# First norm ahead of the embedding projection, output projection beside the last attention blocks, token scales by a three-column chain

## The chip, the cores and the metric

The kernel runs on one core of one Trainium2 chip. The metric is the device time of one execution in microseconds. A core has five engines with an instruction queue each: TensorE (PE) for matmuls, with its weight loads shown apart as PEld; VectorE (DVE); ScalarE (ACT); GpSimd (POOL); and SyncE (SP), which here only issues DMA transfers. They wait for one another through semaphores. Sixteen DMA engines move data between the memory and the core's on-chip buffers. PE writes into PSUM banks; here the large products rotate through one pool of banks (`mm`) and statistics, broadcasts and attention through another (`sm`).

## The reference

One layer of a decoder over 1024 prompt tokens and 32 sample tokens (8 sequences of 4), width 1024, all in float32:

```python
x = x + 0.5 * _swiglu(_rms(x, g1), w1g, w1u, w1d)          # width 1024 -> 2816 -> 1024
z = _rms(x, gm) @ w_in                                     # q | k | v | gate B | gate C | h
q, k = _rms(q, qn), _rms(k, kn)                            # per head of 64
att = sliding window attention (128), 8 query heads, 2 key heads, bias table, sinks
cv  = w_conv[0]*u[t-2] + w_conv[1]*u[t-1] + w_conv[2]*u[t],   u = gate_c * h
x = x + concat([att, gate_b * cv]) @ w_out
x = x + 0.5 * _swiglu(_rms(x, g2), w2g, w2u, w2d)
x = x + sigmoid(_rms(x, gp) @ wpg) * (pe @ wpp)            # pe: embedding of width 256 per token
# _rms(x, g) = x * rsqrt(mean(x*x over the 1024 features) + 1e-6) * g
```

The outputs are x, the last keys and values, and the last two inputs of the convolution.

## The kernel before, in words

Features lie on the 128 partitions in eight tiles `X[0]` to `X[7]`, tokens along the free axis: 1056 columns. So a norm needs a sum over partitions, which PE makes with a matmul against a vector of ones, and its result, one scale for each token, has to be spread over all partitions again. Every float32 operand of a large product is split into a high part (an ACT copy that rounds) and a low part (a DVE subtraction), and a product is three matmuls, high by high, low by high, high by low. The lines 306 to 308 do this for the projections and the down products, 412 to 414 for the gate/up products, 499 to 501 for the first groups of those, 810 to 812 for the embedding projection, 1216 to 1218 for the convolution's columns.

The stages follow one another on PE:

- 0 to 50 us: the embedding projection `pe @ wpp` (`pe_group`, line 806, with PSUM copied out on ACT and DVE, lines 814 and 816); its result is stored and read again at the end. In this stage x is loaded (line 830, one chunk of 528 tokens at a time, two chunks) and chunk 0 is normed: `n_square` (ACT squares x, DVE and POOL add them up, lines 530 to 535), `n_stat` (statistic matmuls on line 548, a chain of small operations for the inverse root on DVE, `small_chain`, lines 232 to 245, broadcast matmuls on line 558, ACT copies on line 559), `n_y` (DVE scales x, line 572, and splits it, lines 334 and 335).
- 50 to 130 us: the first gate/up groups with ordinary products (`lead_group`), fed by chunk 0; the norm of chunk 1 runs beside them as a list of steps, one or two behind each half group. Chunk 1 enters with the third lead group.
- to 520 us the gate/up product by a scheme of seven half-size products, to 795 us the down product.
- 775 to 875 us: the input projection for q, k and v; from here on the tokens are in three chunks (384, 384, 288). Its scales come from `norm_r` (line 281): one statistic matmul per chunk that leaves the sum on all 128 partitions (line 286), and the inverse root on DVE in two halves of the chunk. The same function makes the scales of the final gate at the end.
- 875 to 1117 us: the columns of the convolution (`proj2`), between whose halves the tasks of the sample attention and of the attention blocks 0 to 7 are put by a counter (`half`): scores (1053, 1056), softmax on DVE, ACT and POOL (last operation 1083 on POOL), transposes (1091), product with the values (1100).
- to 1204 us: the output projection (`out_group`, line 1303), its sum with x on DVE (1307). Then the second gate/up (to 1670 us), the second down product (to 1930), and the gate of the embedding with its tanh (`ple`, from line 1362).

An order is written out by hand for each stage; work that is to lie beside another is put in a list by `after(d, fn)`, and `tick()`, called behind each group, runs what is due. `need(flag)` runs the list until a flag is set, `drain()` runs all of it. Weights of the projections pass through two raw buffers (`URAW`) and four split ones: `tick` also splits the next unit as soon as a place is free, and each split starts the load of the next unit on SP. The mixed values (`mix`) of a chunk are split by `split_mix` when its attention blocks are done.

Of the kernel before, what the change touches and what calls it, by code (L numbers as in the profile page):

```python
# [7 lines left out]
F32 = mybir.dt.float32  # L8
# [62 lines left out]
UAT = [40960, 14848, 31680, 33728]  # L71
URAW = [43008, 44032]
# [5 lines left out]
def tile_decoder_layer(  # L78
# [67 lines left out]
    def pump_dma():  # L146
        while st["dma"] < st["end"] and st["dma"] < st["split"] + RAW:
            i = st["dma"]
            t = at("wraw", URAW[i % 2], 1024)
            nc.sync.dma_start(out=t, in_=units[i])  # L150
            raws[i] = t
            st["dma"] += 1
# [128 lines left out]
    def norm_r(c, name, s, d=2):  # L281
        W = CW[c]

        def stat():
            ps = psb(sm)
            nc.tensor.matmul(ps[:, :W], lhsT=ones.broadcast_to([P, P]), rhs=accs[c][:, :W], start=True, stop=True)
            ms = wtile("ms")
            t = wtile("nt")
            rb = rb_of(name, s)[:, CS[c]:CS[c] + W]
            with tc.high_priority(offset=1):  # L290
                nc.vector.tensor_scalar(out=ms[:, :W], in0=ps[:, :W], scalar1=1.0 / D, scalar2=EPS, op0=ALU.mult, op1=ALU.add)
                halves = [slice(0, W // 2), slice(W // 2, W)]
                rsqrt_chain(*[(ms[:, h], rb[:, h], t[:, h]) for h in halves])
            flags.add((name, c))

        after(d, stat)
# [527 lines left out]
    pe_load(praw, psrc, t0_)  # L824
    pe_split(qraw, qh, ql, s0)
    pe_split(praw, ph, pl, t0_)
    pe_load(praw, psrc, t1_)
    pe_load(qraw, wsrc, s1)
    for k in range(KT):
        nc.sync.dma_start(out=chunk(k, 0), in_=xin[:, k, 0:HC])  # L830
    for m in range(4):
        pe_group(m, 0)
    pe_split(praw, ph, pl, t1_)
    for m in range(4):
        pe_group(m, 1)
    pe_split(qraw, qh, ql, s1)
    for k in range(KT):
        n_square(0, k)
    lw1 = lead_weights(w1gu, 0)
    for k in range(KT):  # L840
        nc.sync.dma_start(out=chunk(k, 1), in_=xin[:, k, HC:NT])
    steps0 = chunk0_steps(G1)
    for m in range(4, 8):
        for c in range(2):
            pe_group(m, c)
            if m > 4 and steps0:
                steps0.pop(0)()
    while steps0:
        steps0.pop(0)()

    def chunk1_steps(g, squares):
        s = [lambda k=k: n_square(1, k) for k in range(KT)] if squares else []
        s.append(lambda: n_stat(1))
        return s + [lambda kp=kp, j=j: n_y(1, kp, g, j) for j in range(2) for kp in range(2)]
# [24 lines left out]
    gate_up(w1gu, G1, lw1, chunk1_steps(G1, True), at_end)  # L879
# [4 lines left out]
    mix = [at("mix", KT * CS[c], KT * CW[c]).rearrange("p (k w) -> p k w", k=KT) for c in range(3)]  # L884
# [6 lines left out]
    vsm = at("vsm", 45056, P, rows=NS)  # L891
# [406 lines left out]
    drain()  # L1298
    for k in range(KT):
        nc.sync.dma_start(out=X[k], in_=xm_d[:, k])  # L1300
# [7 lines left out]

    steps0 = chunk0_steps(G2)
    lw2 = None  # L1310
    for c in range(3):
        for m in range(KT):
            out_group(m, c)
            if c == 2:
                wdone(UO + m)
            tick()
            if c == 1:
                n_square(0, m)
                nc.sync.dma_start(out=xs_d[:, m, 0:HC], in_=X[m][:, 0:HC])
            if c == 2:  # L1320
                n_square(1, m)
                nc.sync.dma_start(out=xs_d[:, m, HC:NT], in_=X[m][:, HC:NT])
                if steps0:
                    steps0.pop(0)()
                if m == 4:
                    lw2 = lead_weights(w2gu, 0)
# [19 lines left out]
    gate_up(w2gu, G2, lw2, chunk1_steps(G2, False), dp.early)  # L1346
# [146 lines left out]
```

## Time and profile before

| | |
|---|---|
| median of 3 runs | 2033.95 us (2030.67 to 2036.55) |
| profiled execution | 2031.85 us |
| its span | 2029.9 us, mean granted PE clock 0.984 |
| PE busy | 1986.7 us, 98% of the span, 14051 matmuls |
| DVE, ACT, POOL busy | 1066.5 (53%), 653.2 (32%), 479.3 us (24%) |
| chain of waits that ended last | PE 93%, DVE 5%, ACT 1%, issue 1%, DMA 1% |

The time of the execution is 1.95 us above the span, which runs from the first to the last recorded instruction. Busy time is that of recorded instructions; a busy PE may still run at the lower of its two clocks, which the column of the granted clock tells (1.00 is 2.4 GHz, 0.50 is 1.2 GHz). A row of a timeline can hold several equal instructions (x8); its length then spans all of them.

### The profile page before, as it was taken

The page shows a single profiled execution, that of the slowest core. Times are in us where ns is not written, and L with a number is a line of the kernel's source. Part 1 is how long each engine was busy: PE and PEld are TensorE (multiplying, and loading weights), DVE is VectorE, ACT ScalarE, POOL GpSimd, SP SyncE. Part 2 cuts the span into 40 slices and gives each one's busy share as a digit, 9 for nine tenths or more (in the row PEclk, how much of TensorE's full clock was granted, in tenths as well). Part 3 has the DMA queues.
Part 4 walks back from the last instruction along what each step waited for, and adds up shares of the span by engine and source line. Part 5 has one row for each costly group of instructions (what it writes and reads, how often), then busy time and mean ns, then how long its engine had stood idle before and what let it go on. Part 6 is the DMA issues. An engine that isn't in the chain of part 4 may idle for free.

```text
span 2029.9 us, 34765 instructions
## 1 busy us (share of the span) xinstructions
PE 1986.7 (98%) x14051; PEld 1939.6 (96%) x14051; DVE 1066.5 (53%) x2057; ACT 653.2 (32%) x1334; POOL 479.3 (24%) x414
## 2 busy tenths in 40 slices
PE   7999999999999999999998899999999999999999
PEld 7899999999999999998885899999999999999989
DVE  6745555555524228366684357555555563152474
ACT  5323333334303223323353133333333341042311
POOL 2343343332000122012231025233333310002200
PEclk8999999999999999999997999999999999999999
DMA  7122332221812215111010521223222246121331
GB/s 262 51 84 82 93 115 85 75 85 63 319 56 76 75 60 157 35 30 44 24 30 11 180 86 56 82 86 92 78 82 74 78 145 243 43 76 44 99 106 50
DMA packets 90356, 183.27 MB, mean 90 GB/s; under 512 B 13537, under 2 KB 34921, under 8 KB 90068
## 3 DMA queue, kind: packets, MB, share of 16 engines
q1 hardware_dynamic: 88436, 176.96, 26.5%
q0 software_dynamic: 1472, 4.00, 0.7%
q8 instruction: 110, 1.80, 0.4%
q14 instruction: 50, 0.41, 0.1%
q10 hardware_dynamic: 288, 0.10, 0.0%
HBM read 138.70 MB, written 44.02 MB: 90 GB/s over the span
## 4 chain that ended last, share of the span: by engine, by line
PE 93%; DVE 5%; ACT 1%; issue 1%; DMA 1%; POOL 0%; SPq 0%; ACTq 0%; POOLq 0%; DVEq 0%
PE ps L412 13%; PE ps L413 13%; PE ps L414 13%; PE ps L306 12%; PE ps L307 12%; PE ps L308 12%; PE ps L1217 2%; PE ps L1218 2%; PE ps L1216 2%; PE ps L501 2%; PE ps L499 2%; PE ps L500 2%; PE ps L1056 1%; DVE bl_a L335 1%; PE ps L1053 1%; PE ps L1100 1%
## 5 line engine op out<-in xcount | busy, mean ns | idle before, releaser
L413 PE MATMUL ps<-bh_a,wl_a 128*128 128x264 f32 x2128 | 603.7, 284 | 0.0
L412 PE MATMUL ps<-bh_a,wh_a 128*128 128x264 f32 x2128 | 602.2, 284 | 0.0
L414 PE MATMUL ps<-bl_a,wh_a 128*128 128x264 f32 x2128 | 597.7, 284 | 0.0
L412 PEld LDWEIGHTS ps<-bh_a,wh_a 128*128 128x128 f32 x2128 | 399.9, 188 | 0.6 <-issue 0.6
L413 PEld LDWEIGHTS ps<-bh_a,wl_a 128*128 128x128 f32 x2128 | 399.8, 188 | 0.0
L414 PEld LDWEIGHTS ps<-bl_a,wh_a 128*128 128x128 f32 x2128 | 399.0, 189 | 0.0
L307 PE MATMUL ps<-hh_a,dwl_a 128*128 128x384 f32 (+1 forms) x1056 | 338.8, 321 | 0.0
L306 PE MATMUL ps<-hh_a,dwh_a 128*128 128x384 f32 (+1 forms) x1056 | 337.7, 321 | 0.0
L308 PE MATMUL ps<-hl_a,dwh_a 128*128 128x384 f32 (+1 forms) x1056 | 337.7, 321 | 0.0
L308 PEld LDWEIGHTS ps<-hl_a,dwh_a 128*128 128x128 f32 x1056 | 198.5, 188 | 0.0
L306 PEld LDWEIGHTS ps<-hh_a,dwh_a 128*128 128x128 f32 x1056 | 198.3, 188 | 0.0
L307 PEld LDWEIGHTS ps<-hh_a,dwl_a 128*128 128x128 f32 x1056 | 198.0, 188 | 0.0
L732 DVE SCALAR_TENSOR_TENSOR x_a<-ps,x_a 128x384 f32<-128x384 f32 (+1 forms) x96 | 50.2, 523 | 274.9 <-PE ps L308 270.9
L306 PE MATMUL ps<-xnh_a,whi_a 128*128 128x384 f32 (+1 forms) x528 | 175.2, 332 | 10.5 <-issue 5.7
L307 PE MATMUL ps<-xnh_a,wlo_a 128*128 128x384 f32 (+1 forms) x528 | 172.9, 327 | 1.4 <-DVE wlo_a L161 1.4
L308 PE MATMUL ps<-xnl_a,whi_a 128*128 128x384 f32 (+1 forms) x528 | 172.9, 327 | 0.0
L262 POOL TENSOR_TENSOR acc_a<-acc_a,sq 128x384 f32<-128x384 f32 (+1 forms) x42 | 51.6, 1228 | 436.2 <-ACT sq L261 436.2
L334 ACT CAST wh_a<-ws_a 128x512 fp32r<-128x512 f32 x152 | 94.5, 622 | 155.8 <-PE ps L414 146.4
L335 DVE TENSOR_TENSOR wl_a<-ws_a,wh_a 128x512 fp32r<-128x512 f32 x152 | 107.9, 710 | 58.9 <-ACT wh_a L334 54.2
L335 DVE TENSOR_TENSOR wl_a<-wr_a,wh_a 128x512 fp32r<-128x512 f32 x114 | 105.9, 929 | 30.0 <-ACT wh_a L334 26.3
L306 PEld LDWEIGHTS ps<-xnh_a,whi_a 128*128 128x128 f32 x528 | 101.8, 193 | 14.1 <-issue 7.6
L359 POOL TENSOR_TENSOR ws_a<-wr_a,wr_a 128x512 f32<-128x512 f32 x38 | 52.3, 1377 | 257.9 <-DMA wr_a<-in_w2gu_dram 122.2
(228 smaller groups left out, 3373.2 us busy)
## 6 DMA issues: line engine op xcount, KB each, us to landing
hd<-g_a SPq DMA_DIRECT2D x88, 264.0 KB
wr_a<-in_w1gu_dram SPq DMA_DIRECT2D x88, 256.0 KB
wr_a<-in_w2gu_dram SPq DMA_DIRECT2D x88, 256.0 KB
hr_a<-hd SPq DMA_DIRECT2D x88, 192.0 KB
dwr_a<-in_w1d_dram SPq DMA_DIRECT2D x16, 704.0 KB
dwr_a<-in_w2d_dram SPq DMA_DIRECT2D x16, 704.0 KB
wraw_a<-in_win_dram SPq DMA_DIRECT2D x18, 512.0 KB
hr_a<-hd SPq DMA_DIRECT2D x44, 144.0 KB
```

The lines of the kernel that those rows point to most:

```text
L262: nc.gpsimd.tensor_tensor(out=accs[c], in0=accs[c], in1=sq[:, :W], op=ALU.add)
L306: nc.tensor.matmul(ps[:, :W], lhsT=wh, rhs=xh, start=(k == 0), stop=False)
L307: nc.tensor.matmul(ps[:, :W], lhsT=wl, rhs=xh, start=False, stop=False)
L308: nc.tensor.matmul(ps[:, :W], lhsT=wh, rhs=xl, start=False, stop=(k == n - 1))
L334: nc.scalar.copy(out=hi, in_=src)
L335: nc.vector.tensor_tensor(out=lo, in0=src, in1=hi.bitcast(F32), op=ALU.subtract)
L359: add(out=s[0], in0=r[2], in1=r[3], op=ALU.add)
L412: nc.tensor.matmul(ps[:, :HH], lhsT=wh[:, ks], rhs=bh, start=(start and k == 0), stop=False, skip_group_check=True)
L413: nc.tensor.matmul(ps[:, :HH], lhsT=wl[:, ks], rhs=bh, start=False, stop=False, skip_group_check=True)
L414: nc.tensor.matmul(ps[:, :HH], lhsT=wh[:, ks], rhs=bl, start=False, stop=last, skip_group_check=True)
L499: nc.tensor.matmul(ps[:, :HH], lhsT=wh[:, ks], rhs=bh, start=first, stop=False)
L732: nc.vector.scalar_tensor_tensor(out=x, in0=ps[:, :W], scalar=0.25, in1=x, op0=ALU.mult, op1=ALU.add)
```

## The change

Three things are changed, and buffers are moved for the last of them.

At the start, the eight loads of chunk 0's x are issued ahead of the second half of the embedding operands, every second one from ACT's queue instead of SP's; the squares and the statistic of chunk 0 come ahead of the embedding groups, the scaling of chunk 0 between them; the squares and the sum of chunk 1 come behind the embedding groups and ahead of the lead groups, where they were steps beside the lead groups, and the statistic of chunk 1 (`n_stat(1)`) is the first step.

In `norm_r`, which serves the input projection and the final gate, the sum over partitions now goes to three columns (one matmul for each 128 tokens, tokens on partitions), the inverse root is taken on those three columns by `small_chain`, and three matmuls against the identity and one ACT copy spread the result over all partitions.

At the output projection, `drain()` gives way to `need` for chunk 0 and 1 of the mixed values; the groups run in the order (m 0 to 3, c 0), (0 to 3, c 1), (4 to 7, c 0), (4 to 7, c 1), then chunk 2; x is loaded for m 0 to 4 ahead and for m 5 to 7 before the fifth group. The mixed values of chunk 2, the raw and split weight buffers and one small buffer have new places.

```diff
@@ -68,8 +68,10 @@
     [8448 + 768 * k for k in range(8)],
     [16896 + 576 * k for k in range(8)],
 ]
-UAT = [40960, 14848, 31680, 33728]
-URAW = [43008, 44032]
+UAT = [40512, 14848, 31680, 33728]
+URAW = [42560, 43584]
+URAW2 = [6144, 7168]
+MIXAT = [0, 3072, 42560]
 SLOT = [21504 + 1056 * i for i in range(9)] + [46720, 47776]
 WOUT2 = [21504 + 2048 * i for i in range(4)]
 
@@ -146,7 +148,7 @@
     def pump_dma():
         while st["dma"] < st["end"] and st["dma"] < st["split"] + RAW:
             i = st["dma"]
-            t = at("wraw", URAW[i % 2], 1024)
+            t = at("wraw", (URAW2 if 2 <= i < 26 else URAW)[i % 2], 1024)
             nc.sync.dma_start(out=t, in_=units[i])
             raws[i] = t
             st["dma"] += 1
...
         def stat():
-            ps = psb(sm)
-            nc.tensor.matmul(ps[:, :W], lhsT=ones.broadcast_to([P, P]), rhs=accs[c][:, :W], start=True, stop=True)
-            ms = wtile("ms")
-            t = wtile("nt")
-            rb = rb_of(name, s)[:, CS[c]:CS[c] + W]
-            with tc.high_priority(offset=1):
-                nc.vector.tensor_scalar(out=ms[:, :W], in0=ps[:, :W], scalar1=1.0 / D, scalar2=EPS, op0=ALU.mult, op1=ALU.add)
-                halves = [slice(0, W // 2), slice(W // 2, W)]
-                rsqrt_chain(*[(ms[:, h], rb[:, h], t[:, h]) for h in halves])
+            p2 = psb(sm)
+            ms = small.tile([P, 3], F32, name="pms", tag="pms")
+            r = small.tile([P, 3], F32, name="pr", tag="pr")
+            nc.vector.memset(ms, 1.0)
+            for i, o, n in tiles_of(c):
+                nc.tensor.matmul(p2[:n, i:i + 1], lhsT=accs[c][:, o:o + n], rhs=ones, start=True, stop=True)
+            nf = 3 if c < 2 else 2
+            nc.vector.tensor_scalar(out=ms[:, :nf], in0=p2[:, :nf], scalar1=1.0 / D, scalar2=EPS, op0=ALU.mult, op1=ALU.add)
+            if nf < 3:
+                nc.vector.tensor_scalar(out=ms[:NS, 2:3], in0=p2[:NS, 2:3], scalar1=1.0 / D, scalar2=EPS, op0=ALU.mult, op1=ALU.add)
+            small_chain(ms, r, 3)
+            p3 = psb(sm)
+            for i, o, n in tiles_of(c):
+                nc.tensor.matmul(p3[:, o:o + n], lhsT=r[:n, i:i + 1].broadcast_to([n, P]), rhs=ident[:n, :n], start=True, stop=True)
+            nc.scalar.copy(out=rb_of(name, s)[:, cols(c)], in_=p3[:, :W])
             flags.add((name, c))
 
         after(d, stat)
@@ -822,36 +830,35 @@
     t0_, t1_ = slice(0, HC), slice(HC, NT)
     pe_load(qraw, wsrc, s0)
     pe_load(praw, psrc, t0_)
+    for k in range(KT):
+        (nc.scalar if k % 2 else nc.sync).dma_start(out=chunk(k, 0), in_=xin[:, k, 0:HC])
+    pe_load(praw, psrc, t1_)
+    pe_load(qraw, wsrc, s1)
     pe_split(qraw, qh, ql, s0)
     pe_split(praw, ph, pl, t0_)
-    pe_load(praw, psrc, t1_)
-    pe_load(qraw, wsrc, s1)
+    steps0 = chunk0_steps(G1)
     for k in range(KT):
-        nc.sync.dma_start(out=chunk(k, 0), in_=xin[:, k, 0:HC])
+        n_square(0, k)
+    steps0.pop(0)()
     for m in range(4):
         pe_group(m, 0)
     pe_split(praw, ph, pl, t1_)
+    while steps0:
+        steps0.pop(0)()
+    lw1 = lead_weights(w1gu, 0)
+    for k in range(KT):
+        nc.sync.dma_start(out=chunk(k, 1), in_=xin[:, k, HC:NT])
     for m in range(4):
         pe_group(m, 1)
     pe_split(qraw, qh, ql, s1)
-    for k in range(KT):
-        n_square(0, k)
-    lw1 = lead_weights(w1gu, 0)
-    for k in range(KT):
-        nc.sync.dma_start(out=chunk(k, 1), in_=xin[:, k, HC:NT])
-    steps0 = chunk0_steps(G1)
     for m in range(4, 8):
         for c in range(2):
             pe_group(m, c)
-            if m > 4 and steps0:
-                steps0.pop(0)()
-    while steps0:
-        steps0.pop(0)()
-
-    def chunk1_steps(g, squares):
-        s = [lambda k=k: n_square(1, k) for k in range(KT)] if squares else []
-        s.append(lambda: n_stat(1))
-        return s + [lambda kp=kp, j=j: n_y(1, kp, g, j) for j in range(2) for kp in range(2)]
+    for k in range(KT):
+        n_square(1, k)
+
+    def chunk1_steps(g):
+        return [lambda: n_stat(1)] + [lambda kp=kp, j=j: n_y(1, kp, g, j) for j in range(2) for kp in range(2)]
 
     def mid_hook(m, c):
         square(c, m)
...
-    mix = [at("mix", KT * CS[c], KT * CW[c]).rearrange("p (k w) -> p k w", k=KT) for c in range(3)]
+    mix = [at("mix", MIXAT[c], KT * CW[c]).rearrange("p (k w) -> p k w", k=KT) for c in range(3)]
 
...
-    drain()
-    for k in range(KT):
-        nc.sync.dma_start(out=X[k], in_=xm_d[:, k])
+    def load_xm(ks):
+        for k in ks:
+            nc.sync.dma_start(out=X[k], in_=xm_d[:, k])
...
+    need(("mx", 0))
+    need(("mx", 1))
+    load_xm(range(5))
     steps0 = chunk0_steps(G2)
     lw2 = None
-    for c in range(3):
-        for m in range(KT):
-            out_group(m, c)
-            if c == 2:
-                wdone(UO + m)
-            tick()
-            if c == 1:
-                n_square(0, m)
-                nc.sync.dma_start(out=xs_d[:, m, 0:HC], in_=X[m][:, 0:HC])
-            if c == 2:
-                n_square(1, m)
-                nc.sync.dma_start(out=xs_d[:, m, HC:NT], in_=X[m][:, HC:NT])
-                if steps0:
-                    steps0.pop(0)()
-                if m == 4:
-                    lw2 = lead_weights(w2gu, 0)
+    order = [(m, c) for m0 in (0, 4) for c in (0, 1) for m in range(m0, m0 + 4)] + [(m, 2) for m in range(KT)]
+    for m, c in order:
+        if (m, c) == (0, 1):
+            while st["split"] < 26:
+                split_one()
+            load_xm(range(5, KT))
+        out_group(m, c)
+        if c == 2:
+            wdone(UO + m)
+        tick()
+        if c == 1:
+            n_square(0, m)
+            nc.sync.dma_start(out=xs_d[:, m, 0:HC], in_=X[m][:, 0:HC])
+        if c == 2:
+            n_square(1, m)
+            nc.sync.dma_start(out=xs_d[:, m, HC:NT], in_=X[m][:, HC:NT])
+            if steps0:
+                steps0.pop(0)()
+            if m == 4:
+                lw2 = lead_weights(w2gu, 0)
...
```

The engines' queues move at three places. The first is ACT's queue at the start, before. The names: `wpp` and `pe` (raw `praw`) are the operands of the embedding projection, `po` its result, `x` the activations, `acc` and `sq` their squares, `wh` high parts of the first gate/up weights.

```order
L797 CAST wpph_a_109<-wppr_a_107 128x512
L797 CAST wpph_a_110<-wppr_a_108 128x512
L797 CAST peh_a_103<-praw_a_101 128x528
L797 CAST peh_a_104<-praw_a_102 128x528
L797 CAST peh_a_103<-praw_a_101 128x528
L797 CAST peh_a_104<-praw_a_102 128x528
L797 CAST wpph_a_109<-wppr_a_107 128x512
L797 CAST wpph_a_110<-wppr_a_108 128x512
L814 COPY po_a_113<-ps 128x264
L814 COPY po_a_114<-ps 128x264
L530 ACTIVATE acc<-x_a_72 128x528 x2
L814 COPY po_a_115<-ps 128x264
```

The same place after:

```order
L834 DMA x_a_72<-in_xT_dram 128x528 x4
L805 ACT_TABLE_LOAD
L805 CAST wpph_a_109<-wppr_a_107 128x512
L805 CAST wpph_a_110<-wppr_a_108 128x512
L805 CAST peh_a_103<-praw_a_101 128x528
L805 CAST peh_a_104<-praw_a_102 128x528
L538 ACTIVATE acc<-x_a_72 128x528 x2
L541 ACTIVATE sq<-x_a_72 128x528 x6
L805 CAST peh_a_103<-praw_a_101 128x528
L805 CAST peh_a_104<-praw_a_102 128x528
L822 COPY po_a_113<-ps 128x264
L822 COPY po_a_114<-ps 128x264
```

ACT now issues four loads of x, and the eight squares stand behind four casts and ahead of the four others; before, they stood behind all eight and between the evictions of the first results.

The second place is PE's queue ahead of the transposes (`ident`, `S_a`) of attention block 6, with the buffers' numbers. Before; `ps_10980` is the output group m 3 of chunk 0:

```order
L308 MATMUL ps_10980<-xnl_a45568_6958,whi_a14848_7870 128x384
L306 MATMUL ps_10980<-xnh_a45952_6951,whi_a14848_7870 128x384
L307 MATMUL ps_10980<-xnh_a45952_6951,wlo_a15872_7871 128x384
L308 MATMUL ps_10980<-xnl_a46336_6959,whi_a14848_7870 128x384
L1091 MATMUL ps_10176<-ident_78,S_a25728_9150 128x128 x4
L1091 MATMUL ps_10182<-ident_78,S_a25728_9150 128x128 x4
L1091 MATMUL ps_10201<-ident_78,S_a26784_9153 128x128 x4
L1091 MATMUL ps_10207<-ident_78,S_a26784_9153 128x128 x4
```

The same place after; `ps_11039` is the output group m 1 of chunk 1 (lines 306 to 308 are 314 to 316 there, 1091 is 1098):

```order
L316 MATMUL ps_11039<-xnl_a13440_7819,whi_a33728_8087 128x384
L314 MATMUL ps_11039<-xnh_a13824_7812,whi_a33728_8087 128x384
L315 MATMUL ps_11039<-xnh_a13824_7812,wlo_a34752_8088 128x384
L316 MATMUL ps_11039<-xnl_a14208_7820,whi_a33728_8087 128x384
L1098 MATMUL ps_10176<-ident_78,S_a25728_9150 128x128 x4
L1098 MATMUL ps_10182<-ident_78,S_a25728_9150 128x128 x4
L1098 MATMUL ps_10201<-ident_78,S_a26784_9153 128x128 x4
L1098 MATMUL ps_10207<-ident_78,S_a26784_9153 128x128 x4
```

The group in front of the transposes is now the second one of chunk 1, behind the four groups of chunk 0; before, it was the fourth of chunk 0, so that chunk 1's first two groups have moved ahead of the transposes.

The third place is DVE's queue behind the softmax of block 7, before. `PT` are its transposed weights, `wlo` and `whi` parts of the output weights, `xnl` and `xnh` parts of the last chunk's mixed values, `x` with `ps` is the sum of an output group with x:

```order
L1092 COPY PT_a27840_9233<-ps_10331 128x512
L1092 COPY PT_a28896_9253<-ps_10356 128x512
L161 TENSOR_TENSOR wlo_a22528_10915<-wraw_a43008_7792,whi_a21504_10914 128x1024
L161 TENSOR_TENSOR wlo_a24576_10946<-wraw_a44032_7794,whi_a23552_10945 128x1024
L1231 TENSOR_TENSOR xnl_a17184_7887<-mix_a6144_7952,xnh_a16896_7879 128x288
L1231 TENSOR_TENSOR xnl_a17760_7888<-mix_a6144_7952,xnh_a17472_7880 128x288
L1231 TENSOR_TENSOR xnl_a18336_7889<-mix_a6144_7952,xnh_a18048_7881 128x288
L1231 TENSOR_TENSOR xnl_a18912_7890<-mix_a6144_7952,xnh_a18624_7882 128x288
L161 TENSOR_TENSOR wlo_a26624_10977<-wraw_a43008_7792,whi_a25600_10976 128x1024
L161 TENSOR_TENSOR wlo_a28672_11007<-wraw_a44032_7794,whi_a27648_11006 128x1024
L1307 TENSOR_TENSOR x_a0_72<-x_a0_72,ps_10888 128x384
L1307 TENSOR_TENSOR x_a0_72<-x_a0_72,ps_10919 128x384
```

The same place after (lines 161, 1231 and 1307 are 163, 1238 and 1315 there):

```order
L1099 COPY PT_a27840_9233<-ps_10331 128x512
L1099 COPY PT_a28896_9253<-ps_10356 128x512
L163 TENSOR_TENSOR wlo_a22528_10896<-wraw_a6144_8051,whi_a21504_10895 128x1024
L1238 TENSOR_TENSOR xnl_a17184_7887<-mix_a42560_7952,xnh_a16896_7879 128x288
L1238 TENSOR_TENSOR xnl_a17760_7888<-mix_a42560_7952,xnh_a17472_7880 128x288
L1238 TENSOR_TENSOR xnl_a18336_7889<-mix_a42560_7952,xnh_a18048_7881 128x288
L1238 TENSOR_TENSOR xnl_a18912_7890<-mix_a42560_7952,xnh_a18624_7882 128x288
L1315 TENSOR_TENSOR x_a0_72<-x_a0_72,ps_10904 128x384
L163 TENSOR_TENSOR wlo_a24576_10931<-wraw_a7168_8053,whi_a23552_10930 128x1024
L1315 TENSOR_TENSOR x_a0_72<-x_a0_72,ps_10939 128x384
```

The first sum of an output group now stands behind one weight part and the four splits of `xnl`; before, three more weight parts were ahead of it.


## Rows read from the trace of the kernel before

**Rows 1.** Windows: stretch, length, busy us (xcount) of PE, PEld, DVE, ACT, POOL; clock, DMA, GB/s.

```profile
0.00:25.00 25.00, 21.99 (x140) 21.06 (x141) 15.74 (x34) 15.45 (x28) 5.58 (x8) 0.89 0.96 344
25.00:50.00 25.00, 17.86 (x112) 16.50 (x111) 18.80 (x31) 13.90 (x30) 8.34 (x5) 0.83 0.52 186
50.00:75.00 25.00, 25.00 (x208) 24.63 (x207) 12.41 (x30) 2.92 (x8) 5.50 (x3) 1.00 0.18 67
75.00:100.00 25.00, 21.11 (x144) 20.26 (x143) 25.00 (x36) 12.66 (x24) 10.58 (x6) 0.86 0.10 31
...
800.00:825.00 25.00, 21.95 (x147) 20.79 (x146) 18.63 (x67) 8.09 (x15) 0.00 (x0) 0.93 0.23 65
...
1075.00:1100.00 25.00, 20.58 (x77) 14.01 (x76) 12.56 (x30) 11.28 (x30) 3.79 (x2) 0.76 0.00 0
1100.00:1125.00 25.00, 15.95 (x58) 9.28 (x58) 11.07 (x23) 10.66 (x30) 3.79 (x2) 0.76 0.19 61
1125.00:1150.00 25.00, 22.06 (x115) 22.09 (x116) 7.68 (x13) 2.32 (x5) 0.00 (x0) 0.86 0.68 250
...
1950.00:1975.00 25.00, 21.22 (x115) 21.22 (x116) 17.52 (x36) 6.24 (x11) 0.00 (x0) 0.86 0.47 146
```

**Rows 2.** Timeline, PE, start: begin, length, engine, line, operation; [idle before, releaser].

```profile
50.51 0.29 PE L499 MATMUL ps<-bh_a,wh_a 128*128 128x264 f32 x1
...
81.97 0.59 PE L501 MATMUL ps<-bl_a,wh_a 128*128 128x264 f32 x1 [2.08 <-DVE bl_a L335]
```

**Rows 3.** Timeline of DVE at the start.

```profile
21.92 0.16 DVE L551 TENSOR_SCALAR nms<-ps 128x4 f32<-128x4 f32 x1 [1.78 <-PE ps L548]
...
34.73 7.69 DVE L572 SCALAR_TENSOR_TENSOR x_a<-x_a,vec,rb 128x528 f32<-128x528 f32 x8
...
50.77 0.69 DVE L535 TENSOR_TENSOR acc<-acc,sq 128x528 f32<-128x528 f32 x1
...
74.82 4.17 DVE L572 SCALAR_TENSOR_TENSOR x_a<-x_a,vec,rb 128x528 f32<-128x528 f32 x6 [2.90 <-ACT rb L559]
```

**Rows 4.** Timeline of PE at attention blocks 6 and 7 and behind them.

```profile
1088.86 1.97 PE L1091 MATMUL ps<-ident,S_a 128*128 128x128 f32 x8 [4.09 <-POOL S_a L1083]
...
1100.92 3.68 PE L1100 MATMUL ps<-PT_a,vtm_a 128*64 128x512 f32 x8
...
1109.82 1.97 PE L1091 MATMUL ps<-ident,S_a 128*128 128x128 f32 x8 [4.61 <-POOL S_a L1083]
...
1117.97 0.45 PE L307 MATMUL ps<-xnh_a,wlo_a 128*128 128x384 f32 x1 [1.36 <-DVE wlo_a L161]
...
1127.94 0.66 PE L306 MATMUL ps<-xnh_a,whi_a 128*128 128x384 f32 x1 [5.70 <-issue]
```

**Rows 5.** Timeline of DVE behind the last attention block.

```profile
1119.39 1.56 DVE L1231 TENSOR_TENSOR xnl_a<-mix_a,xnh_a 128x288 fp32r<-128x288 f32 x4
...
1138.62 0.56 DVE L1307 TENSOR_TENSOR x_a<-x_a,ps 128x384 f32<-128x384 f32 x1 [3.61 <-PE ps L308]
...
1142.77 0.55 DVE L1307 TENSOR_TENSOR x_a<-x_a,ps 128x384 f32<-128x384 f32 x1 [3.60 <-PE ps L308]
```

**Rows 6.** Timeline of SP in the same stretch: the loads of x.

```profile
1120.98 5.02 SPq L1300 DMA_DIRECT2D x_a<-xm_d  x8
```

**Rows 7.** Timeline of PE in the input projection.

```profile
807.82 1.24 PE L944 MATMUL ps<-ident,kr 128*64 128x128 f32 x12 [2.70 <-DVE kms L931]
```

**Rows 8.** Timeline of DVE in the input projection.

```profile
816.08 0.17 DVE L238 SCALAR_TENSOR_TENSOR nt<-kr 128x6 f32<-128x6 f32 x1
```

**Rows 9.** Groups by line, PE: xcount, busy us, mean ns, idle before and its releaser.

```profile
L548 PE MATMUL ps<-ones,acc 128*128 128x1 f32 (+1 forms) x96 | 10.4, 226 | 2.7 <-POOL acc L535 2.5 <-DVE acc L535 0.2
...
L558 PE MATMUL ps<-ident,nr 128*128 128x128 f32 (+1 forms) x48 | 7.5, 278 | 0.0
...
L286 PE MATMUL ps<-acc_a,ones 128*128 128x384 f32 (+1 forms) x12 | 4.4, 466 | 0.0
```

**Rows 10.** Waits of PE: idle us, count, longest.

```profile
PE ps L306 <- DVE pth L1366: 4.5, 2, 4.1
```

More of the change, by code (lines that the diff above doesn't have):

```diff
@@ L877, in at_end @@
         dp.early(j, c)
-    gate_up(w1gu, G1, lw1, chunk1_steps(G1, True), at_end)
+    gate_up(w1gu, G1, lw1, chunk1_steps(G1), at_end)
     dp.run()
     st["end"] = 26
-    mix = [at("mix", KT * CS[c], KT * CW[c]).rearrange("p (k w) -> p k w", k=KT) for c in range(3)]
+    mix = [at("mix", MIXAT[c], KT * CW[c]).rearrange("p (k w) -> p k w", k=KT) for c in range(3)]
     U0 = UNIT["win"]
@@ L890, in tile_decoder_layer @@
     vtm = slot(1, [P, 8, P], F32, "vtm")
-    vsm = at("vsm", 45056, P, rows=NS)
+    vsm = at("vsm", 44864, P, rows=NS)
     bias = [slot(2 + kv, [P, 4, 256], F32, f"bias{kv}") for kv in range(2)]
@@ L1345, in tile_decoder_layer @@
     dp = DownProj(w2d, xs_d, ple_hook)
-    gate_up(w2gu, G2, lw2, chunk1_steps(G2, False), dp.early)
+    gate_up(w2gu, G2, lw2, chunk1_steps(G2), dp.early)
     dp.run()
```

## The prediction

> **What bounds the kernel now.** I read the 25 us windows first. Outside the rows shown, TensorE (PE) is busy in the whole of nearly every window at a granted clock of 1.00, as in 50:75 [rows 1]: there nothing but fewer matmuls would help. The time to be had lies in four places. In 25:50 PE is busy 17.86 of 25 us at clock 0.83, in 75:100 21.11 at 0.86, in 800:825 21.95 at 0.93, in 1075:1150 (three rows) 20.58, 15.95 and 22.06 at 0.76, 0.76 and 0.86, in 1950:1975 21.22 at 0.86 [rows 1]. Idle time there is 7.1 + 3.9 + 3.1 + 16.4 + 3.8 = 34.3 us. A clock of 0.86 over 25 us is 3.5 us spent at the lower of the two levels (1.2 instead of 2.4 GHz) beyond what full speed needs, partly inside the idle time. So the change, which touches just these places, can win some 50 us at the very most. Next come the timelines around each hole, to see who releases PE.
>
> **Term 1, the start.** Before, the lead groups of the first gate/up product begin at 50.51 [rows 2], and chunk 1's first use stalls at 81.97 on its split (DVE bl_a) [rows 2], because the scaling of chunk 1 begins only at 74.82 [rows 3]. The change puts the squares of chunk 0 behind four casts instead of behind eight casts and PE's evictions, and the whole sum of chunk 1 (eight squares, the adds, the statistics) ahead of the lead groups.
> The step in front, worked out: the statistic reaches DVE at 21.92 before [rows 3]. After, the squares come earlier, but the remaining splits of the embedding projection and three weight splits now stand in DVE's queue between the adds and the statistic, so I leave it at 21.9. The ten small operations follow each other at about 0.2 us (one takes 0.17, [rows 8]): 24. PE has 30 projection matmuls between statistic and broadcast, at 0.12 us each (208 in 25 us, 50:75 in [rows 1]) or twice that at the lower clock: the broadcast ends near 27. Five squares and two copies on ACT stand before the second half of the scales: the scaling of chunk 0 starts at about 30, against 34.73 [rows 3].
> From there DVE's queue holds the same work as before up to chunk 1's last add, which ended at 50.77 + 0.69 = 51.46, 16.7 us after 34.73 [rows 3]. So it ends at 46.7. Behind it PE still has the statistic of chunk 1 and 30 projection matmuls that wait for evictions in turn: 30 x 0.12 to 30 x 0.24 = 3.6 to 7.2 us, and about 2 for the statistic. Lead groups start at 53.5, 3 us later than before; the 1.9 us of statistic that stood between them are gone, so PE is 1.1 us behind. But chunk 1's scaling follows 29 lead matmuls and the broadcast, near 59, 15.5 us earlier than 74.82, while PE needs chunk 1 only after two lead groups (some 25 us, 79). The hole in 75:100 goes whole: 3.9 idle + 3.5 of clock = 7.4. Net gain 6.3 us. Bounds: lead groups at 59 give 1; at 48.5, 11.
> All 16 loads of x cost the same bytes. In the first 25 us the 16 DMA engines are busy 0.96 of the time at 344 GB/s [rows 1], so a load moved ahead puts another back. The Trainium skill says in "DMA: Bandwidth & Descriptors", section "Issuing engines are not separate DMA queues", that transfers started from several engines interleave on the same 16 engines and that this saves issue time alone. By it the four loads of x that ACT now issues share the wire with the first 1.04 MB that PE waits for, and delay it by some 3 us (1.08 MB at 344 GB/s, an estimate from the row). Were ACT's queue a lane of its own, the scaling would start at 27 and the term be 9. The busy share of the row speaks for the rule.
>
> **Term 2, scales before the input projection.** Before, DVE works two chains of 384 and 288 columns, and PE waits 2.70 us at the key broadcast L944 [rows 7]; with the clock the window 800:825 loses 3.05 + 1.75 = 4.8 us [rows 1]. After, a chain is ten operations of 0.17 on three columns [rows 8]. PE has 40 and 25 matmuls between statistic and broadcast for the last two chunks; at 0.13 to 0.17 us that is 4 us or more against a chain of 2.4, so I see no wait. PE pays: a wide statistic cost 4.4 / 6 = 0.73 us; now three of 10.4 / 48 = 0.22 and three broadcasts of 7.5 / 24 = 0.31 each [rows 9] make 1.59. That is 0.86 more for each of six chunks, 2.6 us per norm. Net gain 4.8 - 2.6 = 2.2. Bounds: 0 (waits stay half as long) to 4.8 (broadcasts lie in idle time).
>
> **Term 3, the last attention blocks.** Before, PE has nothing left at 1088.86 - 4.09 = 1084.77: the transposes of block 6 wait for its softmax [rows 4]. It then does transposes, scores and product of block 6 and 7 at the lower clock, waits 4.61 for block 7 at 1109.82, ends at 1117.97 - 1.36 = 1116.61, waits 1.36 for a weight split, does one group and waits 5.70 until 1127.94, since all PSUM banks hold groups whose x is loaded only from 1120.98 [rows 4, 6].
> After, two groups of chunk 1 stand in front of block 6's transposes; a group takes 1142.77 - 1138.62 = 4.15 us [rows 5]. They run to 1093.1 and cover the first wait, so block 6 and the scores of block 7 run at full clock: from 1088.86 to the end of the product, 1100.92 + 3.68 = 1104.6 [rows 4], 15.7 us become about 9, to 1102.4, with the scores done at 1100.4. Block 7's softmax is not covered: 1109.82 - 1100.92 = 8.9 us from scores to transposes before, which puts them at 1109, 0.8 earlier than before, and 6.8 us later (1109.82 to 1116.61) PE is through at 1115.6. The next group wants the bank of an older one, whose add stands in DVE's queue behind the four splits of the last chunk. Those ended at 1119.39 + 1.56 = 1120.95, 4.3 us after 1116.61 [rows 5]; 1.05 less, since a weight cast now follows them, and 0.55 for the add: 3.7 at most, I take 3.5. PE goes on at 1119.1 with ten groups of chunk 0 and 1 to do. Before, eleven were left at 1127.94. Gain 8.8 + 4.2 = 13; the slow clock after the pause I take as equal. Bounds: 8 (the clock stays low for 10 us longer) to 18 (another pause goes).
>
> **Term 4, scales before the gate of the last product.** Before, PE waits 4.5 us for pth in all, 4.1 of it at once [rows 10], and 1950:1975 loses 3.8 + 3.5 us [rows 1]. After, only 16 matmuls (2.1 us) lie between the last statistic and its broadcast, and a weight split of DVE stands before the first use: 1.8 us of wait and 1.2 of clock remain, and 2.6 of extra PE work. Gain 7.3 - 5.6 = 1.7; bounds -2 to 5.
>
> **The sum.** 6.3 + 2.2 + 13 + 1.7 = 23.2 us. The profiled execution took 2031.85, so 2008.7; the median of the runs is 2.1 above it, which gives 2011. Elsewhere the same instructions run on a PE that was full.
>
> **Rivals.** (a) The start gives nothing: x is loaded earlier, but the first PE work, the evictions and DVE's queue (already 18.80 of 25 us busy in 25:50 [rows 1]) slip as much, and lead groups come at 60. For it: the chain of eight scalings and all splits of chunk 0 is as long as before. Against: chunk 1's sum is out of the way in any case. 2011 + 6 = 2017. (b) The last blocks give half: the add of group 1 stands between two denominators of block 6's softmax on DVE, and if its x came late the transposes would wait. Against: SP issues its load behind no more than two weight loads, well before that block. The term falls to 6: 2018. (c) Slower: PE now stands itself in the norm chains, with six broadcasts in its queue that wait for DVE. Before, a waiting broadcast such as L944 cost 2.70 [rows 7] and the slower clock after it. If each of the six cost 4 us and 3 of clock, 42 us, the result is 2011 + 42 - 2 = 2051. It decides from 23.2 / 6 = 3.9 us for each broadcast on. Against: five of six have 4 us or more of matmuls ahead of them for a chain of 2.4.
>
> **Chances.** A difference under 0.3% (6.1 us) can't be told from none. My own case 0.68, its range 2000 to 2020; (a) 0.13, (b) 0.11, both faster; (c) 0.05; the rest, several terms at their low ends at once, 0.03, within 6 us of before. The range that leaves out 0.2 is 2000 to 2026. Faster 0.90, same 0.05, slower 0.05.
>
> **What will show it.** In the new trace: the statistics of chunk 1 ahead of the first lead matmul, which starts at 52 to 55, and PE full from there to 130. One wait on S_a of POOL of about 6 us instead of two of over 4, the window of block 6 at clock 1.00, and a first wait of about 3.5 us on the x add behind it, none of 5.7. No wait of PE on kms near 808, and broadcasts that PE does not wait for; one wait of some 2 us on pth. The forecast is wrong if lead groups start past 58, if block 6's transposes still wait, or if PE waits for the small chains.

## The result and the profile after

The changed kernel took 2018.59 us (median of 4 runs, 2015.89 to 2020.09); the kernel before, on the same chip, 2032.68. The ratio is 0.9927, interval 0.9907 to 0.9946: 14.8 us faster (11.0 to 18.9). The forecast was 2011 in a range of 2000 to 2026. Direction and range hold; of the 23.2 us forecast, about two thirds came.

The profiled execution took 2015.89 (span 2013.8), 16.0 less than that of before. Where these come from can be read from the first and last start of a line's instructions. In the rows below (line, count, shortest/median/longest in ns, first to last start, shapes), the first is the first gate/up product behind the lead groups, the second the convolution's columns, the third the lead groups of both gate/up products. The kernel before:

```profile
L412 PE MATMUL ps<-bh_a,wh_a x2128: 279/285/387, 132.4 to 1677.1; 128*128 128x264 f32 x194
...
L1216 PE MATMUL ps<-xnh_a,whi_a x288: 292/334/445, 863.7 to 1058.7; 128*128 128x384 f32 x96, 128*128 128x288 f32 x48
...
L499 PE MATMUL ps<-bh_a,wh_a x384: 279/285/422, 50.5 to 1282.0; 128*128 128x264 f32 x192
```

The same lines of the changed kernel:

```profile
L420 PE MATMUL ps<-bh_a,wh_a x2128: 279/285/388, 128.1 to 1661.6; 128*128 128x264 f32 x194
...
L1223 PE MATMUL ps<-xnh_a,whi_a x288: 290/334/445, 857.7 to 1052.6; 128*128 128x384 f32 x96, 128*128 128x288 f32 x48
...
L507 PE MATMUL ps<-bh_a,wh_a x384: 279/283/387, 55.8 to 1266.4; 128*128 128x264 f32 x192
```

Behind the start the kernel is 4.3 us ahead (132.4 to 128.1), at the convolution 6.0, at the end of the second lead groups 15.6, at the end of the span 16.1. So in this one pair of executions the start gave 4.3, the first scales 1.7, the last blocks 9.6, the last scales 0.5. The windows of after that answer to [rows 1]:

```profile
0.00:25.00 25.00, 17.97 (x118) 17.27 (x119) 14.41 (x34) 13.57 (x25) 5.57 (x8) 0.86 0.94 338
25.00:50.00 25.00, 18.32 (x125) 16.88 (x123) 21.70 (x36) 14.14 (x31) 9.45 (x6) 0.86 0.55 181
50.00:75.00 25.00, 25.00 (x192) 24.44 (x192) 20.25 (x39) 11.51 (x24) 9.59 (x7) 0.93 0.17 66
75.00:100.00 25.00, 25.00 (x207) 25.00 (x206) 19.28 (x29) 7.38 (x16) 13.84 (x9) 1.00 0.23 76
800.00:825.00 25.00, 24.90 (x181) 23.69 (x180) 13.81 (x49) 10.41 (x21) 0.00 (x0) 1.00 0.15 47
1075.00:1100.00 25.00, 22.93 (x110) 17.50 (x108) 12.38 (x34) 10.14 (x33) 3.79 (x2) 0.86 0.29 109
1100.00:1125.00 25.00, 15.63 (x61) 12.20 (x62) 8.50 (x15) 7.98 (x22) 3.78 (x2) 0.67 0.28 84
1125.00:1150.00 25.00, 25.00 (x146) 25.00 (x145) 9.23 (x15) 4.54 (x7) 1.33 (x1) 1.00 0.46 150
1925.00:1950.00 25.00, 23.00 (x140) 22.44 (x141) 16.56 (x48) 6.92 (x12) 0.00 (x0) 0.93 0.46 137
1950.00:1975.00 25.00, 25.00 (x161) 25.00 (x159) 12.88 (x23) 4.89 (x8) 0.00 (x0) 1.00 0.14 48
```

Two of the holes are shut: 75:100 and 800:825 are full, or nearly so, at clock 1.00. The one at the last gate has moved ahead with its stage and shrunk: 1925:1950 is now 23.00 at 0.93 and 1950:1975 full. Before, 1950:1975 was 21.22 at 0.86 [rows 1] and the window ahead of it

```profile
1925.00:1950.00 25.00, 24.31 (x146) 23.21 (x144) 20.04 (x64) 3.67 (x7) 1.62 (x1) 1.00 0.31 117
```

Two places are no better. At the start, 25:50 is about as empty as before (18.32 against 17.86), and in 0:25 PE now does 118 matmuls where it did 140. And 1100:1125 is as empty as before, at a lower clock (0.67 against 0.76). The timeline of PE says what ends the waits there (begin, length, operation, idle before and releaser):

```profile
8.95 0.59 PE L818 MATMUL ps<-peh_a,wpph_a 128*128 128x264 f32 x1 [3.59 <-ACT peh_a L805]
...
39.69 0.59 PE L818 MATMUL ps<-peh_a,wpph_a 128*128 128x264 f32 x1 [4.29 <-DVE po_a L824]
...
1086.89 2.04 PE L1098 MATMUL ps<-ident,S_a 128*128 128x128 f32 x16
...
1103.16 1.97 PE L1098 MATMUL ps<-ident,S_a 128*128 128x128 f32 x8 [5.22 <-POOL S_a L1090]
...
1107.35 3.15 PE L1107 MATMUL ps<-PT_a,vtm_a 128*64 128x512 f32 x8
1116.10 0.69 PE L314 MATMUL ps<-xnh_a,whi_a 128*128 128x384 f32 x1 [5.59 <-DVE x_a L1315]
```

The transposes of block 6, at 1086.89, wait no longer [rows 4]. Block 7's wait 5.22, and behind its product PE waits 5.59 for the sum of an output group with x. DVE's timeline at that place:

```profile
1111.72 1.56 DVE L1238 TENSOR_TENSOR xnl_a<-mix_a,xnh_a 128x288 fp32r<-128x288 f32 x4
1115.49 0.56 DVE L1315 TENSOR_TENSOR x_a<-x_a,ps 128x384 f32<-128x384 f32 x1 [2.21 <-DMA wraw_a<-in_wout_dram]
1117.15 1.23 DVE L163 TENSOR_TENSOR wlo_a<-wraw_a,whi_a 128x1024 fp32r<-128x1024 f32 x1 [1.11 <-ACT whi_a L162]
1122.05 0.56 DVE L1315 TENSOR_TENSOR x_a<-x_a,ps 128x384 f32<-128x384 f32 x1 [3.67 <-DMA wraw_a<-in_wout_dram]
```

Behind the splits DVE is idle: the sum waits 2.21 us for the load of a weight unit, the next one 3.67 for the load after it, though a sum reads no weights. SP issued these two loads at

```profile
1111.88 0.33 SPq L152 DMA_DIRECT2D wraw_a<-in_wout_dram  x1
...
1118.41 0.33 SPq L152 DMA_DIRECT2D wraw_a<-in_wout_dram  x1
```

The scales do what was forecast. Statistics and broadcasts cost PE 4.4 + 5.3 = 9.7 us against 4.4 [rows 9], 0.88 more for each of six; no wait on kms is left, and the wait on pth is 1.9 (before 4.5 [rows 10], forecast 1.8):

```profile
L300 PE MATMUL ps<-ident,pr 128*128 128x128 f32 (+1 forms) x36 | 5.3, 277 | 0.1
L292 PE MATMUL ps<-ones,acc_a 128*128 128x1 f32 (+1 forms) x36 | 4.4, 234 | 0.0
```

### The profile page after: what moved, and what is told of

Read it like the earlier page. It is cut to its first block, busy times and chain, and to the rows that moved or that the text cites. A ratio compares the mean times of both kernels' runs of the same rounds, so it can differ in the third digit from the quotient of the medians.

```text
span 2013.8 us, 34845 instructions
## 1 busy us (share of the span) xinstructions
PE 1981.3 (98%) x14111; PEld 1937.9 (96%) x14111; DVE 1041.7 (52%) x2005; ACT 655.3 (33%) x1340; POOL 478.0 (24%) x414
## 4 chain that ended last, share of the span: by engine, by line
PE 96%; DVE 2%; DMA 1%; ACT 1%; issue 0%; POOL 0%; SPq 0%; ACTq 0%; DVEq 0%; POOLq 0%
PE ps L420 13%; PE ps L421 13%; PE ps L422 13%; PE ps L314 13%; PE ps L315 13%; PE ps L316 13%; PE ps L1225 2%; PE ps L1224 2%; PE ps L1223 2%; PE ps L509 2%; PE ps L508 2%; PE ps L507 2%; PE ps L1063 1%; PE ps L1107 1%; PE ps L1060 1%; PE ps L1098 1%
## 5 line engine op out<-in xcount | busy, mean ns | idle before, releaser
L693 ACT CAST dwh_a<-dwr_a 128x1408 fp32r<-128x1408 f32 x32 | 43.9, 1373 | 208.4 <-PE ps L316 196.1
```

The costliest lines, as they stand in the source:

```text
L693: nc.scalar.copy(out=hi, in_=raw)
```

## The experiments

Gains below are in us of about 2032, from the ratio to the kernel before with its interval. The first three runs each make one part of the change alone.

**The start alone (e1).** The hunk at the embedding projection and `chunk1_steps`, nothing else.

> The kernel before with the start alone changed (loads of x, squares and sums ahead; nothing else). Theory A (the parts add up, each with what the new trace shows at its place): the first gate/up product behind the lead groups starts 4.3 us earlier than before (132.4 to about 128), its lead groups about 5 us later (55.8), and the whole is 4.3 us faster, ratio 0.998. Theory B (the start as forecast, 6.3, and something later in the full change takes 2 us back): 6.3 us faster, ratio 0.997, lead groups at 53.5. Theory C (the start gives nothing by itself): within 1 us of before.

Measured: ratio 0.9995 (0.9983 to 1.0008), a gain of 1.0 (-1.6 to 3.5). That is Theory C. The lead groups begin at 60.5 in the profiled execution, with the clock at 0.80 and 0.86 in these windows:

```profile
25.00:50.00 25.00, 18.50 (x119) 17.51 (x119) 19.86 (x36) 13.76 (x30) 7.97 (x5) 0.80 0.45 154
50.00:75.00 25.00, 24.16 (x174) 23.36 (x173) 18.91 (x40) 9.99 (x21) 7.13 (x4) 0.86 0.25 94
```

The full change, with the same code there, began them at 55.8, and e4 at 56.7: executions of one start differ by 4.7 us. The 4.3 read from one pair above is therefore no good measure of this part; the ratio over 12 runs is a better one.

**The token scales alone (e2).** The hunk in `norm_r`.

> The kernel before with the token scales alone changed (three statistic columns, small chain, three broadcasts, in the input projection and in the last gate). Theory A: 1.7 us ahead of the input projection's end and 0.4 us at the last gate, 2.1 us together, ratio 0.999. Theory B (as forecast): 2.2 + 1.7 = 3.9 us, ratio 0.998. Theory C (PE's extra matmuls, 0.86 us for each of six, eat all of it): 0 to 2 us slower. In the trace no wait of PE on kms near 808 by A and B.

Measured: 0.9988 (0.9979 to 0.9998), a gain of 2.4 (0.4 to 4.3). Theory A's 2.1 fits best; the interval does not exclude B's 3.9, and it excludes C. No wait on kms, pth 1.9, as in the full change.

**The output projection alone (e3).** The hunks at `drain()`, the order, and the places of the buffers.

> The kernel before with the output projection alone changed (order of the groups, need instead of drain, places of the buffers). Theory A: 9.6 us faster, ratio 0.9953, with the two waits of the full change behind block 7 (about 5 on the softmax, about 5.6 on the sum with x). Theory B (as forecast, 13): ratio 0.9936. Theory C (the order gives less without the shifted stages ahead of it): under 6 us.

Measured: 0.9947 (0.9933 to 0.9960), a gain of 10.8 (8.1 to 13.6). Theory A's 9.6 is nearest, and its two waits are there; the interval excludes C, but not B's 13. PE waits 5.22 on the softmax of block 7 and 5.79 on the sum, as in the full change. The three parts make 1.0 + 2.4 + 10.8 = 14.2, the full change 14.8: they add up.

**What the sum waits for (e4).** The program says which completion counters an instruction waits for. In the changed kernel, the sum of group m 1 and the ACT cast of the raw weights at 6144 wait for the same one, DMAHW5:

```
L1315 TENSOR_TENSOR x_a0_72<-x_a0_72,ps_10904 128x384 [waits DMAHW5_49,DVE_49]
L162 CAST whi_a25600_10965<-wraw_a6144_8051 128x1024 [waits DMASW3_49,DMASW2_49,DMASW4_49,DMASW1_49,DMASW7_49,DMASW0_49,DMAHW5_49,DVE_49,Pool_49]
```

The counters are few and are used in turn, so that one name alone proves little; but both wait for the same count of it, and the row of 1115.49 above names a weight load as what ended the wait. X[1] lies at columns 1056 to 2111, the raw buffer at 6144, but all eight x tiles are one tensor of 8448 columns, and `URAW2` lies inside it. In e4 the tiles are two tensors at the same addresses:

```diff
+    X4[:] = [at(n, 4 * i * NT, 4 * NT).rearrange("p (k t) -> p k t", k=4) for i, n in enumerate(("xlo", "xhi"))]
+    X[:] = [X4[k // 4][:, k % 4] for k in range(KT)]
...
-    load_xm(range(5))
+    load_xm(range(4))
```

The same sum then waits for the load of its own x alone (`xlo_a0_10860<-xlo_a0_10860,ps_10905 128x384 [waits DMAHW1_49]`).

> The full change, but the eight x tiles of the output projection are two tensors of four tiles each at the same addresses, so that the sums of the first four tiles share no tensor with the bytes under the raw weight buffers (the fifth tile is loaded with the last three). Theory A: in the full change the sums wait for the load of a weight unit that they do not use, because the raw buffers lie inside the one x tensor; here they run as soon as their group and their x are there, banks come free, more groups stand ahead of block 7's transposes, the wait of 5.59 on the sum goes, and the wait on the softmax falls to 3 or 4: 7 to 11 us faster than the full change, 2007 to 2012. Theory B (the second wait is DVE's queue of splits ahead of the sums, whatever the tensors): no more than 2.2 us faster, the idle time in front of the first sum, 2016. Theory C (more groups ahead delay the softmax chain as much as they cover): same time as the full change.

Measured: 2008.06 us, 0.9878 (0.9861 to 0.9895), a gain of 24.8, some 10 more than the full change by the ratios (7.8 by the spans of the two profiled executions, 2013.8 and 2006.0): Theory A. PE's waits at the last blocks in e4:

```profile
1111.54 1.97 PE L1099 MATMUL ps<-ident,S_a 128*128 128x128 f32 x8 [4.60 <-POOL S_a L1091]
...
1119.21 0.45 PE L316 MATMUL ps<-xnh_a,wlo_a 128*128 128x384 f32 x1 [1.36 <-DVE wlo_a L164]
```

No wait for a sum is left; a split of 1.36 comes in its place. All eight sums of the first four x tiles now run ahead of block 7's transposes. And 1075:1125 holds 25.00 + 18.72 us of busy PE at 1.00 and 0.86 (22.93 + 15.63 at 0.86 and 0.67 in the full change):

```profile
1075.00:1100.00 25.00, 25.00 (x142) 22.46 (x139) 13.20 (x31) 10.24 (x29) 5.12 (x3) 1.00 0.32 120
1100.00:1125.00 25.00, 18.72 (x87) 13.46 (x86) 13.07 (x27) 11.49 (x30) 4.34 (x2) 0.86 0.20 59
```

The wait on the softmax fell less than expected (4.60, expected 3 to 4).

**Chunk 1's sum alone (f4).** The kernel before with one part of the start:

```diff
     while steps0:
         steps0.pop(0)()
+    for k in range(KT):
+        n_square(1, k)
...
-    gate_up(w1gu, G1, lw1, chunk1_steps(G1, True), at_end)
+    gate_up(w1gu, G1, lw1, chunk1_steps(G1, False), at_end)
```

> The kernel before with one part of the start alone: the squares and the sum of chunk 1 behind the embedding groups, ahead of the lead groups, and nothing else (chunk 0's loads, squares and scaling as before). Theory A (the hole at 75:100 is this part's to fill, and the rest of the start costs what it wins): the wait on bl near 82 and the slower clock behind it go, 4 to 6 us faster than before (2026 to 2028), better than the whole start by itself. Theory B (the sum of chunk 1 puts the lead groups back by as much): within 1.5 us of before, as the whole start was.

Measured: 0.9963 (0.9949 to 0.9978), a gain of 7.5 (4.5 to 10.4): Theory A. The first gate/up product starts at 124.6, PE is nearly full in 50:100, and the lead groups are not late (49.3):

```profile
50.00:75.00 25.00, 25.00 (x208) 24.50 (x207) 21.12 (x38) 10.80 (x22) 11.99 (x7) 1.00 0.13 50
75.00:100.00 25.00, 24.72 (x200) 24.31 (x200) 19.69 (x29) 7.06 (x14) 11.65 (x8) 1.00 0.20 64
```

So the other part of the start, chunk 0's loads, squares and scaling ahead of the embedding groups, costs 7.5 - 1.0 = 6.5 us. By the two intervals that is 6.5 give or take some 4, an estimate.

**Who issues the loads of x (f1).** e4 with all eight loads of chunk 0 on SP:

```diff
-        (nc.scalar if k % 2 else nc.sync).dma_start(out=chunk(k, 0), in_=xin[:, k, 0:HC])
+        nc.sync.dma_start(out=chunk(k, 0), in_=xin[:, k, 0:HC])
```

> As e4, but all eight loads of chunk 0's x are issued by SP, none by ACT. Theory A (ACT's 4.2 us of issuing hold its table load and the first casts): the first embedding matmul comes at 6.8 to 7.5 instead of 8.7 to 9.0. Theory B (the wire: the x loads share the 16 engines with the operands that PE waits for): it stays at 8.5 or later. On the time: if the start's gain is lost in those 2 us, 2 us faster than e4 (2006); if what counts is the chain of sums and scalings behind, the later loads of x cost as much as is won: 2008, as e4.

Measured: 0.9873 (0.9859 to 0.9887); PE's first embedding matmul at 6.39 instead of 8.69 in e4 and 8.95 in the full change. The place is the one that Theory A gives, but the run can't tell A from B: with SP issuing the loads of x behind the operands, their transfers no longer lie beside those of the operands either. On the time, 1.0 us from e4, the intervals don't separate 2 from 0. The queues behind also came out in another order: in f1 the first copies of po stand between ACT's squares, in the full change behind them. ACT's queue in the full change:

```profile
1.66 4.24 ACTq L834 DMA_DIRECT2D x_a<-in_xT_dram  x4
5.94 1.28 ACT L805 ACT_TABLE_LOAD   x1 [5.94 <-DMA ident<-in_ident_dram]
7.23 1.14 ACT L805 CAST wpph_a<-wppr_a 128x512 fp32r<-128x512 f32 x2
8.27 0.63 ACT L805 CAST peh_a<-praw_a 128x528 fp32r<-128x528 f32 x1
9.19 0.64 ACT L805 CAST peh_a<-praw_a 128x528 fp32r<-128x528 f32 x1 [0.29 <-DMA praw_a<-in_peT_dram]
10.60 1.18 ACT L538 ACTIVATE acc<-x_a 128x528 f32<-128x528 f32 x2 [0.78 <-DMA x_a<-in_xT_dram]
```

and in f1:

```profile
1.66 1.28 ACT L806 ACT_TABLE_LOAD   x1 [1.66 <-PEq L1492]
3.75 0.62 ACT L806 CAST wpph_a<-wppr_a 128x512 fp32r<-128x512 f32 x1 [0.80 <-DMA wppr_a<-in_wpp_dram]
...
5.70 0.63 ACT L806 CAST peh_a<-praw_a 128x528 fp32r<-128x528 f32 x1 [0.27 <-DMA praw_a<-in_peT_dram]
7.06 0.63 ACT L806 CAST peh_a<-praw_a 128x528 fp32r<-128x528 f32 x1 [0.72 <-DMA praw_a<-in_peT_dram]
7.77 1.34 ACT L539 ACTIVATE acc<-x_a 128x528 f32<-128x528 f32 x2
```

Four loads hold ACT 4.24 us. Without them the casts begin 3.5 us earlier and the squares 2.8 (7.77; 10.60 in the full change), though half the loads are issued later. But most of the 4.24 is not the issuing. The four loads by themselves, in the full change (shortest/median/longest in ns):

```profile
L834 ACTq DMA_DIRECT2D x_a<-in_xT_dram x4: 334/394/454, 1.7 to 5.6; - x4
```

That is 1.6 us; in the other 2.7 ACT waits between them. The program gives each load a completion counter, in turn, and a load whose counter an older load still holds waits until that one has landed: by the program ACT's third load waits for the first load of `wpp` and its fourth for that of `ident`, which the row of 5.94 names too.

The casts of `pe` show the other half. SP issues the first two loads of `praw` in the same 0.91 us from 1.65 on in both kernels. The second of them is there at 9.19 in the full change, with ACT's loads of x beside it (9.37 in e4), and at 7.06 in f1, where all loads of x come behind it: the transfers beside it delay it by some 2.1 us. So both theories have a part. The first cast of `pe` (8.27) follows ACT's own queue without a wait, the second (9.19) waits for the wire. What each would cost without the other no run shows.

**The copies behind the scalings (f2).** e4 with `if h or 4 < pn[0] <= 8:` in `pe_group`, so that ACT copies both halves of four groups.

> As e4, but in the four embedding groups of chunk 1 both halves are copied out of PSUM by ACT, none by DVE (which does the other groups' first halves as before). Theory A (the start's gain is lost where PE waits for a copy that stands in DVE's queue behind eight scalings of 7.6 us): the wait of 4.3 on po of DVE goes or falls under 1.5, the lead groups begin at 51 to 53 instead of 55.8 to 60.5, and the time is 3 to 5 us under e4: 2003 to 2005. Theory B (ACT's queue with squares and casts is as full there): the wait moves to ACT, gain under 1.5 us. Theory C (the splits of the scaled chunk bind the lead groups in any case): the wait goes, the lead groups wait for bl instead, gain under 1.5 us.

Measured: 0.9883 (0.9866 to 0.9900), no gain over e4. The wait of 4.3 is gone, the longest on DVE's copies is 2.2, but ACT's copies now cost 4.5 us in four waits, and the lead groups begin at 59.2: Theory B.

**Both (f3).**

> Both edits of f1_sp and f2_act. If the two effects are independent, the time is e4 less the sum of their gains (between 2001 and 2008); if one chain binds, no better than the better of the two.

Measured: 2002.84 us, 0.9856 (0.9842 to 0.9870), 4.5 us better than e4, lead groups at 52.1. Neither edit alone shows a gain that can be told from none, both together most of the 6.5. That they cover for each other is likely, since each leaves a wait that the other takes; it isn't shown, for the intervals of f3 and e4 overlap a little, and the order of the queues changed too.

**The start of f4 in the mended kernel (g1).** e4 with the start of the kernel before and chunk 1's sum ahead of the lead groups.

> As e4 (the full change with the x tiles in two tensors), but the start of the kernel before with one part of the change: chunk 1's squares and sum ahead of the lead groups; chunk 0's loads, squares and scaling where they were. Theory A (the parts add up, and moving chunk 0's norm ahead of the embedding groups costs what chunk 1's sum wins): e4 at 0.9878 less the 0.9963 to 0.9995 between f4 and e1, some 6.5 us: 0.9846, 2001 to 2002. Theory B (moving chunk 0's norm costs nothing once the last blocks are mended): as e4, 2007 to 2008.

Measured: 2002.75 us (2001.95 to 2004.32), 0.9857 (0.9840 to 0.9874): 4.3 us better than e4, between the theories and nearer to A, whose 0.9846 the interval holds; B's 0.9878 lies just outside, though e4's own interval overlaps. The 4.3 is a second measure of what f4 and e1 put at 6.5: the cost of moving chunk 0's norm. With f3 the fastest kernel here, 29 us under before and some 14 under the full change.

## Why the prediction was right, and which step failed

- **Faster, and inside the range:** right. The holes and the parts were the right ones, though of the 23.2 us only 14.8 came: the start fell short by some 5, the last blocks by 2, the scales by 1.5. Rival (c) (slower, by PE in the norm chains) did not come: PE waits for the new broadcasts 0.1 us in all. Of the prediction's own signs two failed: the wait on the x add, put at 3.5, came as 5.59, and the lead groups, put at 52 to 55, came at 55.8. The time by itself is no proof of the case: 2018.59 is nearest to the 2017 and 2018 of rivals (a) and (b), and only the runs of the parts tell these apart.
- **Term 2 and 4, the scales:** forecast 2.2 + 1.7 = 3.9, alone 2.4 (0.4 to 4.3). PE's price (0.86 forecast, 0.88 measured) and the wait on pth were right. The interval holds the forecast, so no step of it can be called wrong.
- **Term 3, the last blocks:** forecast 13, alone 10.8 (8.1 to 13.6). The first wait went, block 6 no longer waits, block 7's transposes come at 1103.16, which with the 6.0 us won ahead of the convolution is the 1109 forecast. (Its sum has two slips: 1109 + 6.8 is 1115.8, not 1115.6, and 4.3 - 1.05 + 0.55 is 3.8, not 3.7.) The step that was off is "I take 3.5" for the wait behind the product: it is 5.59. I counted the splits in DVE's queue, and the sum as ready behind them; it waited 2.21 more for a weight load, since the raw buffers had been moved under the x tensor. e4 shows that this wait and the groups it kept back cost some 10 us.
- **Term 1, the start: the step that failed.** Forecast 6.3, alone 1.0 (-1.6 to 3.5). The gain was sized well: the hole at 75:100 was put at 7.4, and chunk 1's sum alone brings 7.5. What failed is the cost, 1.1 us net for "lead groups start at 53.5, 3 us later than before". They came at 55.8, 56.7 and 60.5 in three executions, and the move of chunk 0 costs 6.5 (4.3 by g1 against e4). The traces show two places where the cost arises. PE's first matmul comes 2.2 us later (8.95; 6.79 before), behind ACT's 4.24 us at the loads and operands that land later; I had read ACT's queue for its order, put no time on its loads, and left the statistic at 21.9 all the same. And PE waits 4.29 for a copy that stands in DVE's queue behind the eight scalings:

```profile
23.35 0.15 DVE L559 TENSOR_SCALAR nms<-ps 128x4 f32<-128x4 f32 x1
...
31.05 7.64 DVE L580 SCALAR_TENSOR_TENSOR x_a<-x_a,vec,rb 128x528 f32<-128x528 f32 x8
38.61 0.68 DVE L389 TENSOR_TENSOR wl_a<-wr_a,wh_a 128x512 fp32r<-128x512 f32 x1
39.22 0.42 DVE L824 COPY po_a<-ps 128x264 f32<-128x264 f32 x1
```

The statistic put at 21.9 came at 23.35, the scaling put at 30 at 31.05 here and at 34.25 in e1. How the cost divides among these stays open: f1 and f2, which take one each, show no gain. Rival (a), that the start gives nothing, was the right one for this term, with 0.13.

- **The wire.** I let the x loads delay the operands by some 3 us on the shared wire, by the Trainium skill, "DMA: Bandwidth & Descriptors", section "Issuing engines are not separate DMA queues", which says that loads started from several engines interleave on the same 16 DMA engines. The trace agrees: the second operand tile of `pe` lands 2.1 us later with ACT's loads beside it (9.19) than in f1 (7.06). The delay stands in the prediction's text, but not in its sum. The Trainium skill also says there that a second issuing engine saves issue time; no saving is seen here: with their waits, four loads on ACT take 4.24 us and the four on SP beside them 4.59, the eight on SP alone in f1 4.79.

## What to carry to other kernels

A DMA that is moved to a compute engine's queue holds that engine at the place where it stands, here 4.24 us for four: 1.6 of issuing, the rest waits for older loads whose counters they take. Its bytes also delay the operands that are under way, here by 2.1 us. Price both, like any instruction in front of what waits. When a buffer is moved, look for every tensor that it now overlaps: in this program the wait is made for the whole tensor, not for the columns used. Test the parts of a change alone, since a part that wins 7.5 and one that loses 6.5 look like one that does nothing.

## What was not expected of the hardware

Executions of the same start differ by up to 4.7 us at the first lead group (55.8 to 60.5), with the granted clock in 25:50 at 0.86 and 0.80. Four loads held ACT 4.24 us, though each is issued in 0.33 to 0.45. SP's queue has such waits too: its eight loads of x took 5.64 before, with ACT issuing none of them:

```profile
5.01 5.64 SPq L830 DMA_DIRECT2D x_a<-in_xT_dram  x8
```
